# Down projection wholly by seven half-size products, one tile for weight sums, accumulation in DRAM

## The chip, the cores and the metric

One core of one Trainium2 chip runs one launch of the kernel. The metric is device time in microseconds (us).

## The reference

A decoder layer on 512 tokens of width 2048 with an MLP of width 8192, in float32. Cut to what matters:

```python
x = x + jnp.concatenate([attn, ssm], axis=-1) @ w_out[i]
x = x + cross_attention(rms_norm(x, g_cross[i]), rms_norm(mem, g_mem[i]), ...)
hm = rms_norm(x, g_mlp[i])
x = x + jnp.square(jax.nn.relu(hm @ w_up[i])) @ w_down[i]
```

`attn` is a dilated-window attention, `ssm` a chunked state-space scan (SSD); both come out of one input projection of `x`.

## The kernel before, in words

**Arithmetic.** Every float32 operand is split in a high and a low float32r part (ACT copies the high part, DVE subtracts it to get the low one), and a product is three matmuls: high by high, high by low, low by high. For plain products these are lines L212 to L214 (`mm3`), with rows of 512 columns.

**Seven products.** The up projection doesn't multiply 2x2 blocks by eight half-size products but by seven, from sums of the blocks of either operand (Strassen's scheme in Winograd's form). These matmuls have 256 columns (L920 to L922, `up_products`). The operands' sums have to be made and split too: of the weights in `up_forms` (L894 to L911), of the activations in `forms`; the seven results are put together in `combine` (L924), seven DVE operations.

**Stages.** In order of time: input projection, attention and SSD, up to about 690 us; W_out and the cross attention, up to about 1040 us; the up projection, 32 groups `f` of 256 columns, four steps each, a step being the 512 KB of weights that one DMA brings, up to 1666 us; the down projection, up to 2347 us.

**The up projection's step.** SP loads a raw tile `wr` (three buffers, L891). ACT copies three of its four blocks to `wh` (L899), DVE makes four sums of 256 columns (L901 to L904) in `sw`, ACT copies those to `sh` (L905), DVE subtracts: L908 gives `wl` (768 columns), L909 gives `sl` (1024 columns). `wh`, `wl`, `sh`, `sl` have two buffers each. PE then issues 42 matmuls. After four steps ACT copies one of the seven results out of PSUM (L930), DVE combines (L932 to L938), ACT applies relu and square and stores to DRAM.

**The down projection's step.** Its 8192 rows are cut in 8 chunks. Of the 2048 output columns, 0 to 1023 go by seven products (four groups S0 to S3, two steps of 42 matmuls each) and 1024 to 2047 by plain products (two groups P0 and P1 of 512 columns, four steps of 24 matmuls each): 16 steps in a chunk, 128 in all. The list `steps` gives the order. Sums over chunks stay in SBUF: S groups in `accs` by DVE additions (L1128), P groups in `acc`, which starts as the residual from DRAM (`x3d`), by a DVE operation that also scales by the row factor `c2` (L1117). After the last chunk the S groups are combined, transposed on PE (L1158), scaled, added to the residual (L1159) and stored (L1160). A step loads the weights of the step after next (`load_step`), prepares those of the next (`prep_step`), empties the banks of the last (`evac_step`), and multiplies (`mm_step`).

**Memory pools.** `wp` holds the raw, high and low weight tiles of the whole kernel; `bq` holds the 12 scratch tiles (`q`) of attention and SSD and is closed after SSD (`mixer.close()`); `wq`, with the sums of the weights, is opened after that in the place of `bq`. `bp` has the 68 general tiles `b`.

**What sets the order.** A scheduler orders each engine's instructions when the kernel is built; on the chip each engine then runs its own list in that order and waits at the head of it. `weights` has a raised priority (`PRI`).

Of the kernel before, what the change touches and what calls it, by code (L numbers as in the profile page):

```python
# [18 lines left out]
NT = 4  # L19
# [4 lines left out]
DS = 1024  # L24
# [52 lines left out]
def pack_up(w):  # L77


    k, m = w.shape  # L80
    t = w.reshape(k // 512, 2, 2, 128, m // 256, 2, 128).transpose(4, 0, 3, 5, 2, 1, 6)
    return np.ascontiguousarray(np.stack([t[:, :, :, 1, 0], t[:, :, :, 0, 0], t[:, :, :, 0, 1], t[:, :, :, 1, 1]], axis=3))


def pack(inputs):
# [18 lines left out]
        "wds": pack_up(inputs["w_down"][0][:, :DS]),  # L104
        "wdp": pack_rows(inputs["w_down"][0][:, DS:], 512),
# [4 lines left out]
def tile_layer(ctx, tc, vec, x, xT, memT_d, pos, wqk, wv0, wv1, wv2, wzx, wout, wcq, wckv, wco, wup, wds, wdp,  # L110
               out):
# [4 lines left out]
    wp = ctx.enter_context(tc.tile_pool(name="wp", bufs=2))  # L116
# [6 lines left out]
    bq = mixer.enter_context(tc.tile_pool(name="bq", bufs=NBUFQ))  # L123

# [71 lines left out]
    def load(src):  # L196
        a, n = src.shape[1], src.shape[2]
        raw = wp.tile([128, 1024], F32, name="wr", tag="wr", bufs=WR)[:, :a * n]
        nc.sync.dma_start(h3(raw, a), src)
        return raw, a, a * n  # L200

    def weights(src):
        with tc.high_priority(PRI):
            raw, a, n = src if isinstance(src, tuple) else load(src)
            hi = wp.tile([128, 1024], F32R, name="wh", tag="wh", bufs=WH)[:, :n]
            lo = wp.tile([128, 1024], F32R, name="wl", tag="wl", bufs=WH)[:, :n]
# [53 lines left out]
    first = wp.tile([128, 1024], F32, name="wr", tag="wr", bufs=WR)  # L260
# [403 lines left out]
    wq = ctx.enter_context(tc.tile_pool(name="wq", bufs=WQ, reuse_waits="tile"))  # L664
# [7 lines left out]
    x3d = dp.tile([4, 4, 128, 512], F32, name="x3d")  # L672
# [198 lines left out]
    def third_out(n, xr, ps):  # L871
        xs = []
        for t in range(NT):
# [3 lines left out]
            act.dma_start(x3d[t, n], xr[t])  # L877
# [8 lines left out]
    prods = ((0, 0, 0, H0), (1, 1, 0, H1), (2, 6, 1, H0), (3, 3, 1, H1), (4, 4, 2, H0), (5, 5, 2, H1), (6, 2, 3, H0))  # L886
    adr = [dp.tile([128, 512], F32, name=f"a{f}") for f in range(FF // 128)]

    def up_weights(f, q, w=wup):
        raw = wp.tile([128, 1024], F32, name="wr", tag="wr", bufs=WR)  # L890
        nc.sync.dma_start(raw, w[f, q].rearrange("p a b c -> p (a b c)"))  # L891
        return raw

    def up_forms(raw):  # L894
        w21, w11, w12, w22 = (raw[:, 256 * i:256 * i + 256] for i in range(4))
        hi = wp.tile([128, 1024], F32R, name="wh", tag="wh", bufs=WH)
        sw = wq.tile([128, 1024], F32, name="sw", tag="sw")
# [323 lines left out]
```

## Time and profile before

| | before |
|---|---|
| median of 3 runs | 2354.26 us (2353.75 to 2355.12) |
| profiled execution, its own time | 2353.13 us |
| its span, first to last instruction | 2351.1 us |
| PE busy | 2338.1 us, 99% |
| DVE busy | 1686.9 us, 72% |
| ACT busy | 1118.5 us, 48% |
| POOL busy | 13.4 us |
| DMA | 286 MB, 122 GB/s mean |
| mean granted TensorE clock | 1.000 |

PE is the TensorE matmul, PEld its weight load, DVE the VectorE, ACT the ScalarE, POOL the GpSimd, SP the SyncE, which here only issues DMAs. A granted clock of 1.000 is the full 2.4 GHz. Busy shares are means over all stages.

### The profile page before, as it was taken

How to read it: one execution, taken by the hardware profiler on the slowest of the kernel's cores; microseconds unless marked ns; L12 is line 12 of the kernel's file. 1: busy time of each engine (PE TensorE's matmuls, PEld its weight loads, DVE VectorE, ACT ScalarE, POOL GpSimd, SP SyncE). 2: the span in 40 equal slices, each digit the busy share in tenths (PEclk: the TensorE clock that was granted, in tenths of full speed). 3: DMA queues.
4: the chain of work that ended last, by engine and by line, in shares of the span. 5: the costliest groups of instructions: out<-in, count | busy, mean ns of one | idle time of the engine just before them, and what ended most of it. 6: DMA issues, size and time to landing. Idle time of an engine off the chain costs nothing.

```text
span 2351.1 us, 36723 instructions
## 1 busy us (share of the span) xinstructions
PE 2338.1 (99%) x14606; PEld 2077.8 (88%) x14606; DVE 1686.9 (72%) x3100; ACT 1118.5 (48%) x1722; POOL 13.4 (1%) x30
## 2 busy tenths in 40 slices
PE   9999999999999999999999999999999999999999
PEld 8889977777778887789999999999988989889898
DVE  7544276686673346688888888888867887887787
ACT  6334277655452346675444444554543443443332
POOL 0000000000000000000000000000000000000000
PEclk9999999999999999999999999999999999999999
DMA  5222321122224456434443444444543433343344
GB/s 198 90 87 80 99 66 59 54 72 81 74 81 133 160 167 202 135 108 135 133 128 129 132 135 135 131 131 135 187 137 119 140 127 109 132 135 119 117 135 144
DMA packets 98283, 286.22 MB, mean 122 GB/s; under 512 B 11200, under 2 KB 15424, under 8 KB 98112
## 3 DMA queue, kind: packets, MB, share of 16 engines
q1 hardware_dynamic: 82368, 252.42, 33.3%
q10 hardware_dynamic: 13824, 25.17, 2.8%
q0 software_dynamic: 1920, 6.29, 0.9%
q8 instruction: 114, 1.87, 0.3%
q14 instruction: 57, 0.47, 0.1%
HBM read 254.48 MB, written 29.36 MB: 121 GB/s over the span
## 4 chain that ended last, share of the span: by engine, by line
PE 95%; ACT 2%; DVE 2%; issue 1%; DMA 0%; SPq 0%; ACTq 0%; DVEq 0%
PE mm L214 13%; PE mm L212 13%; PE mm L213 13%; PE aux L922 7%; PE mm L922 7%; PE aux L920 7%; PE mm L920 7%; PE aux L921 7%; PE mm L921 7%; PE aux L213 3%; PE aux L214 3%; PE aux L212 3%; PE aux L248 1%; PE aux L523 1%; PE aux L514 1%
## 5 line engine op out<-in xcount | busy, mean ns | idle before, releaser
L208 DVE TENSOR_TENSOR wl<-wr,wh 128x1024 fp32r<-128x1024 f32 (+2 forms) x223 | 264.4, 1186 | 281.7 <-ACT wh L207 280.9
L207 ACT ACTIVATE wh<-wr 128x1024 fp32r<-128x1024 f32 (+2 forms) x223 | 229.3, 1028 | 458.3 <-PE mm L214 250.3
L212 PE MATMUL mm<-wh,b 128*128 128x512 f32 (+2 forms) x1056 | 404.8, 384 | 3.3 <-ACT b L422 1.6
L213 PE MATMUL mm<-wl,b 128*128 128x512 f32 (+2 forms) x1056 | 402.8, 382 | 0.9 <-DVE wl L208 0.7
L214 PE MATMUL mm<-wh,b 128*128 128x512 f32 (+2 forms) x1056 | 402.6, 381 | 0.0
L899 ACT ACTIVATE wh<-wr 128x768 fp32r<-128x768 f32 x192 | 162.5, 846 | 309.4 <-PE mm L921 121.4
L909 DVE TENSOR_TENSOR sl<-sw,sh 128x1024 fp32r<-128x1024 f32 x192 | 234.5, 1221 | 97.1 <-ACT sh L905 96.8
L905 ACT ACTIVATE sh<-sw 128x1024 fp32r<-128x1024 f32 x192 | 203.6, 1061 | 120.3 <-DVE sw L904 37.1
L212 PEld LDWEIGHTS mm<-wh,b 128*128 128x128 f32 x1056 | 198.7, 188 | 42.9 <-ACT b L422 2.0
L213 PEld LDWEIGHTS mm<-wl,b 128*128 128x128 f32 x1056 | 198.8, 188 | 39.8 <-DVE wl L208 2.1
L214 PEld LDWEIGHTS mm<-wh,b 128*128 128x128 f32 x1056 | 198.7, 188 | 38.1 <-issue 0.2
L921 PE MATMUL mm<-b,sh 128*128 128x256 f32 x768 | 217.2, 283 | 0.0
L921 PE MATMUL aux<-b,sh 128*128 128x256 f32 x768 | 217.2, 283 | 0.0
L920 PE MATMUL mm<-b,sh 128*128 128x256 f32 x768 | 217.2, 283 | 0.0
L920 PE MATMUL aux<-b,sh 128*128 128x256 f32 x768 | 217.2, 283 | 0.0
L922 PE MATMUL mm<-b,sl 128*128 128x256 f32 x768 | 216.9, 283 | 0.0
L922 PE MATMUL aux<-b,sl 128*128 128x256 f32 x768 | 216.6, 283 | 0.0
L908 DVE TENSOR_TENSOR wl<-wr,wh 128x768 fp32r<-128x768 f32 x192 | 183.3, 955 | 26.9 <-ACT wh L899 19.8
L922 PE MATMUL aux<-b,wl 128*128 128x256 f32 x576 | 162.1, 282 | 1.2 <-DVE wl L908 1.1
L920 PE MATMUL mm<-b,wh 128*128 128x256 f32 x576 | 162.4, 282 | 0.0
L920 PE MATMUL aux<-b,wh 128*128 128x256 f32 x576 | 162.2, 282 | 0.0
L922 PE MATMUL mm<-b,wl 128*128 128x256 f32 x576 | 162.1, 281 | 0.0
(303 smaller groups left out, 5252.2 us busy)
## 6 DMA issues: line engine op xcount, KB each, us to landing
wr<-in_wup_dram SPq DMA_DIRECT2D x128, 512.0 KB, 3.8
wr<-in_wdp_dram SPq DMA_DIRECT2D x64, 512.0 KB, 3.7
wr<-in_wds_dram SPq DMA_DIRECT2D x64, 512.0 KB, 3.7
wr<-in_wzx_dram SPq DMA_DIRECT2D x48, 512.0 KB, 3.6
wr<-in_wout_dram SPq DMA_DIRECT2D x32, 512.0 KB, 3.8
a<-b ACTq DMA_DIRECT2D x64, 256.0 KB, 4.6
b<-a SPq DMA_DIRECT2D x64, 256.0 KB, 4.4
wr<-in_wqk_dram SPq DMA_DIRECT2D x31, 512.0 KB, 3.6
```

The source lines that it names most:

```text
L207: act.activation(hi, raw, AF.Copy)
L208: dve.tensor_tensor(lo, raw, hi.bitcast(F32), OP.subtract)
L212: pe.matmul(ps, l[0], r[0], start=start, stop=False)
L213: pe.matmul(ps, l[0], r[1], start=False, stop=False)
L214: pe.matmul(ps, l[1], r[0], start=False, stop=stop)
L899: act.activation(hi[:, :768], raw[:, 256:], AF.Copy)
L905: act.activation(shi, sw, AF.Copy)
L908: dve.tensor_tensor(lo[:, :768], raw[:, 256:], hi[:, :768].bitcast(F32), OP.subtract)
L909: dve.tensor_tensor(slo, sw, shi.bitcast(F32), OP.subtract)
L920: pe.matmul(ps[b][:, H], w[0][:, d], xf[0], start=st, stop=False, skip_group_check=True)
L921: pe.matmul(ps[b][:, H], w[0][:, d], xf[1], start=False, stop=False, skip_group_check=True)
L922: pe.matmul(ps[b][:, H], w[1][:, d], xf[0], start=False, stop=sp_, skip_group_check=True)
```

## The change

1. **Down projection.** All eight groups of 256 output columns go by seven products. A chunk has 8 groups of two steps; all 128 steps have 42 matmuls of 256 columns. The plain path is gone. The last two groups of the up projection (f = 30 and 31) are interleaved step by step.
2. **Weights.** `wp` and `wq` give way to one pool `zp`, opened after `mixer.close()`, hence in the memory of `wp` and `bq`: `zr` (three raw tiles of 2048 columns), `zh` and `zl` (two each, 1792 columns). `wp` itself now closes with `mixer`, so that W_out and all later weights use `zr`, `zh`, `zl`. The sums are made in `zr` beside the raw blocks by one add of 512 columns with a broadcast input (L903) and two of 256 (L904, L905). ACT copies 768 (L902) and 1024 columns (L906), and one DVE operation of 1792 columns subtracts all (L907).
3. **Partial sums.** ACT copies the seven results' four banks to SBUF (L1104); GpSimd DMAs add them into `accd` in DRAM (L1106; the first chunk stores, L1108). In the last chunk groups 0 to 5 are read back, combined, transposed (L1143), scaled by ACT (L1144) and added by GpSimd DMAs (L1145) into `out`, where `third_out` has already put the residual; `x3d` is gone. The last two groups (`LATE`) read `accd` early and add on DVE (L1100).
4. **Combination.** `combine` has five DVE operations in place of seven (two of 512 columns with a broadcast input; L928 to L930, L850), and the activations' sums are made by fewer, wider ones.

The core of the diff:

```diff
+    wp = mixer.enter_context(tc.tile_pool(name="wp", bufs=2))
...
     mixer.close()
-    wq = ctx.enter_context(tc.tile_pool(name="wq", bufs=WQ, reuse_waits="tile"))
+    zp = ctx.enter_context(tc.tile_pool(name="zp", bufs=2, reuse_waits="tile"))
+    weight_tile.update(raw=lambda: zp.tile([128, 2048], F32, name="zr", tag="zr", bufs=WR),
+                       hi=lambda: zp.tile([128, 1792], F32R, name="zh", tag="zh", bufs=WH),
+                       lo=lambda: zp.tile([128, 1792], F32R, name="zl", tag="zl", bufs=WH))
...
     def up_forms(raw):
-        act.activation(hi[:, :768], raw[:, 256:], AF.Copy)
-        dve.tensor_tensor(s1, w21, w22, OP.add)
-        dve.tensor_tensor(s2, s1, w11, OP.subtract)
-        dve.tensor_tensor(s3, w11, w21, OP.subtract)
-        dve.tensor_tensor(s4, w12, s2, OP.subtract)
-        act.activation(shi, sw, AF.Copy)
-        dve.tensor_tensor(lo[:, :768], raw[:, 256:], hi[:, :768].bitcast(F32), OP.subtract)
-        dve.tensor_tensor(slo, sw, shi.bitcast(F32), OP.subtract)
+        act.activation(hi[:, 1024:], q(4, 3), AF.Copy)
+        dve.tensor_tensor(h3(q(2, 2), 2), h3(q(4, 2), 2), q(7)[:, None, :].to_broadcast([128, 2, 256]), OP.add)
+        dve.tensor_tensor(q(1), q(2), q(5), OP.add)
+        dve.tensor_tensor(q(0), q(1), q(6), OP.add)
+        act.activation(hi[:, :1024], q(0, 4), AF.Copy)
+        dve.tensor_tensor(lo, q(0, 7), hi.bitcast(F32), OP.subtract)
...
+    def combine(b, copy):
+        dve.tensor_tensor(h3(t1, 2), h3(b[1], 2), p1[:, None, :].to_broadcast([128, 2, 256]), OP.add)
+        dve.tensor_tensor(h3(t2, 2), h3(b[2], 2), t1[:, None, H1].to_broadcast([128, 2, 256]), OP.add)
+        dve.tensor_tensor(t1[:, H1], b[0][:, H1], t2[:, H1], OP.add)
+        stt_(t3[:, H0], t2[:, H0], b[2][:, H1])
+        stt_(t3[:, H1], t2[:, H0], b[3][:, H0])
...
+    steps = [("U", 0, f, q, 4) for q in range(4) for f in (NU - 2, NU - 1)]
+    steps += [("S", c, j, q, FCH // 512) for c in range(NC) for j in range(NJ) for q in range(FCH // 512)]
...
+        elif c == NC - 1 and j >= NJ - LATE:
+            for b, w in enumerate(BW):
+                dve.tensor_tensor(accs[j][b][:, w], ps[b][:, w], accs[j][b][:, w], OP.add)
         else:
+            for b, w in enumerate(BW):
+                o = big()
+                act.activation(o[:, w], ps[b][:, w], AF.Copy)
                 if c:
+                    nc.gpsimd.dma_start(accd[j][b], o[:, w], accum_op=OP.add)
                 else:
+                    nc.gpsimd.dma_start(accd[j][b], o[:, w])
...
+            act.activation(r[:, h], p[:, h], AF.Copy, scale=c2[:, t:t + 1])
+            nc.gpsimd.dma_start(out[t * 128:t * 128 + 128, j * 256:j * 256 + 256], r[:, h], accum_op=OP.add)
```

**Order on PE at the end of SSD.** Before, L640 and L644 (the last block's products) stand among W_out's matmuls (L212 to L214 from `wh`, `wl`):

```order
L640 MATMUL aux<-q 64x128
L212 MATMUL mm<-wh,b 128x512 x3
L213 MATMUL mm<-wl,b 128x512
L214 MATMUL mm<-wh,b 128x512
L213 MATMUL mm<-wl,b 128x512
L640 MATMUL aux<-q 64x128 x3
L644 MATMUL aux<-q 64x128 x2
L640 MATMUL aux<-q 64x128 x2
L644 MATMUL aux<-q 64x128 x2
L640 MATMUL aux<-q 64x128 x2
L644 MATMUL aux<-q 64x128 x2
L214 MATMUL mm<-wh,b 128x512
```

Of the change, the same place:

```order
L608 MATMUL aux<-q,b 128x128 x3
L620 MATMUL aux<-acsT,sel 128x512 x2
L640 MATMUL aux<-q 64x128 x4
L644 MATMUL aux<-q 64x128 x2
L640 MATMUL aux<-q 64x128 x2
L644 MATMUL aux<-q 64x128 x2
L640 MATMUL aux<-q 64x128 x2
L644 MATMUL aux<-q 64x128 x2
L578 MATMUL aux<-b,ones 128x512
L212 MATMUL mm<-zh,b 128x512 x4
L213 MATMUL mm<-zl,b 128x512
L214 MATMUL mm<-zh,b 128x512
```

No matmul of W_out stands ahead of the last SSD product now. The first load of a `zr` tile waits for the last reading of the scratch tiles `q`.

**Order on DVE in the up projection**, of one step f to the next. Before (L901 to L904 sums, L908 and L909 subtractions, L932 to L938 combination; the numbers tell tiles apart):

```order
L932 TENSOR_TENSOR b_12125<-mm_11892,b_12127 128x256
L908 TENSOR_TENSOR wl_12214<-wr_12203,wh_12205 128x768
L933 TENSOR_TENSOR b_12124<-mm_11894,b_12127 128x256
L934 TENSOR_TENSOR b_12124<-mm_11894,b_12124 128x256
L909 TENSOR_TENSOR sl_12215<-sw_12206,sh_12207 128x1024
L935 TENSOR_TENSOR b_12124<-mm_11893,b_12124 128x256
L936 TENSOR_TENSOR b_12126<-mm_11893,b_12124 128x256
L937 TENSOR_TENSOR b_12126<-mm_11893,b_12124 128x256
L938 TENSOR_TENSOR b_12125<-mm_11895,b_12124 128x256
L901 TENSOR_TENSOR sw_12320<-wr_12317 128x256
L903 TENSOR_TENSOR sw_12320<-wr_12317 128x256
L908 TENSOR_TENSOR wl_12271<-wr_12260,wh_12262 128x768
```

Of the change (L903 to L905 sums, L907 the subtraction, L930 and L850 the end of the combination):

```order
L929 TENSOR_TENSOR b_11116<-aux_10905,b_11115 128x512
L907 TENSOR_TENSOR zl_11189<-zr_11186,zh_11188 128x1792
L930 TENSOR_TENSOR b_11115<-aux_10903,b_11116 128x256
L850 SCALAR_TENSOR_TENSOR b_11117<-b_11116,aux_10905 128x256
L850 SCALAR_TENSOR_TENSOR b_11117<-b_11116,aux_10906 128x256
L903 TENSOR_TENSOR zr_11290<-zr_11290 128x512
L904 TENSOR_TENSOR zr_11290<-zr_11290 128x256
L905 TENSOR_TENSOR zr_11290<-zr_11290 128x256
L903 TENSOR_TENSOR zr_11361<-zr_11361 128x512
L904 TENSOR_TENSOR zr_11361<-zr_11361 128x256
L905 TENSOR_TENSOR zr_11361<-zr_11361 128x256
L907 TENSOR_TENSOR zl_11241<-zr_11238,zh_11240 128x1792
```

The tile zr_11361 is the third raw tile after zr_11186, so it has the same buffer, which L907 on zr_11186 (second row) releases. Its sums (L903 to L905) stand ahead of the subtraction that gives zl_11241, the next tile that PE needs. Before, the sums that stand ahead of L908 on wr_12260 are those of the next tile, wr_12317, whose buffer was released a step earlier.

**Order on DVE in the down projection**, of the change, in the first chunk (L187: low parts of activations):

```order
L903 TENSOR_TENSOR zr_19914<-zr_19914 128x512
L187 TENSOR_TENSOR b_19801<-b_19784,b_19800 128x512
L904 TENSOR_TENSOR zr_19914<-zr_19914 128x256
L905 TENSOR_TENSOR zr_19914<-zr_19914 128x256
L903 TENSOR_TENSOR zr_19970<-zr_19970 128x512
L904 TENSOR_TENSOR zr_19970<-zr_19970 128x256
L907 TENSOR_TENSOR zl_19917<-zr_19846,zh_19916 128x1792
L905 TENSOR_TENSOR zr_19970<-zr_19970 128x256
L907 TENSOR_TENSOR zl_19973<-zr_19914,zh_19972 128x1792
```

Again sums of a tile two steps on (zr_19970) stand ahead of the subtraction that gives zl_19917. There are four such places in a chunk of 16 steps.

## Rows read from the trace of the kernel before

**Rows 1.** The page: busy times, and the chain that ended last.
```profile
PE 2338.1 (99%) x14606; PEld 2077.8 (88%) x14606; DVE 1686.9 (72%) x3100; ACT 1118.5 (48%) x1722; POOL 13.4 (1%) x30
...
PE 95%; ACT 2%; DVE 2%; issue 1%; DMA 0%; SPq 0%; ACTq 0%; DVEq 0%
```

**Rows 2.** Timeline of PE, down projection: start, duration (us), engine, line, operation.
```profile
1679.66 0.39 PE L212 MATMUL mm<-wh,b 128*128 128x512 f32 x1
...
1687.79 0.40 PE L214 MATMUL mm<-wh,b 128*128 128x512 f32 x1
1688.03 0.28 PE L920 MATMUL aux<-b,wh 128*128 128x256 f32 x1
...
1689.94 0.28 PE L921 MATMUL aux<-b,sh 128*128 128x256 f32 x1
```

**Rows 3.** Line L930 alone: the copy that follows each up-projection column group.
```profile
L930 ACT ACTIVATE b<-mm x16: 384/384/385, 1044.1 to 1644.1; 128x256 f32<-128x256 f32 x16
```

**Rows 4.** Busy time by window, up projection: PE, PEld, DVE, ACT, POOL, clock, DMA share, GB/s.
```profile
1200.00:1400.00 200.00, 200.00 (x1683) 200.00 (x1682) 166.88 (x311) 99.95 (x131) 0.00 (x0) 1.00 0.41 132
```

**Rows 5.** Lines by form, us 662.8 to 686.1: the last SSD blocks.
```profile
L212 PE MATMUL mm<-wh,b 128*128 128x512 f32 x20 | 8.2, 426 | 0.9 <-ACT wh L207 0.9
L213 PE MATMUL mm<-wl,b 128*128 128x512 f32 x18 | 7.2, 400 | 0.2 <-DVE wl L208 0.2
L214 PE MATMUL mm<-wh,b 128*128 128x512 f32 x17 | 6.8, 400 | 0.0
...
L208 DVE TENSOR_TENSOR wl<-wr,wh 128x1024 fp32r<-128x1024 f32 x4 | 4.9, 1216 | 0.0
```

**Rows 6.** Timeline of us 682 to 696: last SSD product.
```profile
685.68 0.48 PE L644 MATMUL aux<-q 128*64 128x128 f32 x3
```

**Rows 7.** Lines by form, us 1200 to 1600, up projection.
```profile
L909 DVE TENSOR_TENSOR sl<-sw,sh 128x1024 fp32r<-128x1024 f32 x80 | 97.8, 1222 | 52.0 <-ACT sh L905 52.0
...
L905 ACT ACTIVATE sh<-sw 128x1024 fp32r<-128x1024 f32 x80 | 84.9, 1061 | 45.7 <-PE aux L921 18.3 <-PE mm L921 18.1 <-ACT b L944 8.1
L908 DVE TENSOR_TENSOR wl<-wr,wh 128x768 fp32r<-128x768 f32 x80 | 76.6, 957 | 11.8 <-ACT wh L899 7.2
L899 ACT ACTIVATE wh<-wr 128x768 fp32r<-128x768 f32 x81 | 68.6, 847 | 112.7 <-PE mm L921 57.5 <-PE aux L921 55.0
...
L902 DVE TENSOR_TENSOR sw<-sw,wr 128x256 f32<-128x256 f32 x81 | 33.8, 418 | 0.0
```

**Rows 8.** Lines by form, us 620 to 700: an add whose second input is broadcast.
```profile
L602 DVE TENSOR_TENSOR q<-aux,dt 128x512 f32<-128x512 f32 x3 | 2.1, 684 | 2.3 <-PE aux L248 2.3
```

**Rows 9.** Timelines of SP and DVE, us 1788 to 1817; brackets: idle before, releaser.
```profile
1793.69 18.58 SPq L891 DMA_DIRECT2D wr<-in_wds_dram  x4
...
1797.42 0.42 DVE L901 TENSOR_TENSOR sw<-wr 128x256 f32<-128x256 f32 x1 [2.83 <-DMA wr<-in_wds_dram]
```

**Rows 10.** Timeline of ACT and DVE, us 1199 to 1225.
```profile
1204.12 0.38 ACT L930 ACTIVATE b<-mm 128x256 f32<-128x256 f32 x1 [2.22 <-PE mm L922]
...
1209.41 0.41 DVE L901 TENSOR_TENSOR sw<-wr 128x256 f32<-128x256 f32 x1
```

**Rows 11.** DMA issues of the line L891, us 1200 to 1600.
```profile
DMA to landing us min/median/max: 3.3/3.8/6.0
```

**Rows 12.** Lines by form, us 1750 to 2300, down projection.
```profile
L901 DVE TENSOR_TENSOR sw<-wr 128x256 f32<-128x256 f32 x55 | 23.1, 421 | 45.2 <-DMA wr<-in_wds_dram 45.2
```

**Rows 13.** DMA queues, us 1200 to 1600: packets, MB, share of 16 engines.
```profile
q1 hardware_dynamic: 11520, 41.95, 34.1%
q10 hardware_dynamic: 5760, 10.49, 6.8%
```

**Rows 14.** DMA issues by POOL, us 700 to 1200.
```profile
L868 POOL DMA_DIRECT2D b<-x2d x16 | 8.5, 538 | 111.9 <-PE mm L214 70.5 <-PE aux L248 20.5 <-PE mm L834 12.0
```

**Rows 15.** Timeline of us 2326 to 2352: the last DVE operation.
```profile
2347.13 0.75 DVE L1117 SCALAR_TENSOR_TENSOR b<-aux,c,b 128x512 f32<-128x512 f32 x1 [0.65 <-PE aux L214]
```

**Rows 16.** The page, DMA issues: KB each, median us from issue to landing.
```profile
out_dram<-b SPq DMA_DIRECT2D x16, 128.0 KB, 2.0
```

More of the change, by code (lines that the diff above doesn't have):

```diff
@@ L197, in load @@
         a, n = src.shape[1], src.shape[2]
-        raw = wp.tile([128, 1024], F32, name="wr", tag="wr", bufs=WR)[:, :a * n]
+        raw = weight_tile["raw"]()[:, :a * n]
         nc.sync.dma_start(h3(raw, a), src)
@@ L259, in tile_layer @@
     pos_i = cp.tile([128, 4], I32, name="pos_i")
-    first = wp.tile([128, 1024], F32, name="wr", tag="wr", bufs=WR)
+    first = weight_tile["raw"]()
     ahead.append((first, 2, 1024))
@@ L278, in split_h @@
         if i == 0:
-            hi = wp.tile([128, 1024], F32R, name="wh", tag="wh", bufs=WH)
-            lo = wp.tile([128, 1024], F32R, name="wl", tag="wl", bufs=WH)
+            hi = weight_tile["hi"]()
+            lo = weight_tile["lo"]()
             ahead[0] = h3(hi, 2), h3(lo, 2)
@@ L913, in up_bank @@
+        act.activation(hi[:, :1024], q(0, 4), AF.Copy)
+        dve.tensor_tensor(lo, q(0, 7), hi.bitcast(F32), OP.subtract)
+        return [tuple(h3(a[:, 256 * i:256 * i + 256], 2) for a in (hi, lo)) for i in range(7)]
     def up_bank(f):
@@ L1053, in tile_layer @@
     dve.tensor_tensor(c2, c2, v2, OP.mult)
-    LAST = FF // 256 - 1
-    for f in range(1, LAST):
+    NU = FF // 256
+    for f in range(1, NU - 2):
         ps = up_bank(f)
@@ L1063, in tile_layer @@
         up_out(f, ps)
[L1067 to L1075 removed]
+    NC, NP, NJ = FF // FCH, FCH // 256, D // 256
+    steps = [("U", 0, f, q, 4) for q in range(4) for f in (NU - 2, NU - 1)]
+    US = len(steps)
+    steps += [("S", c, j, q, FCH // 512) for c in range(NC) for j in range(NJ) for q in range(FCH // 512)]
+    raws, wts, banks, accs = {}, {}, {}, {}
+    araw, AF_ = {}, {}
+    tags = [0]
+    accd = [[dp.tile([128, 512 if b < 3 else 256], F32, name=f"acc{j}_{b}") for b in range(4)] for j in range(NJ)]
+    BW = [slice(0, 512)] * 3 + [H0]
     def load_step(i):
@@ L1147, in cols_sum @@
     def cols_sum(j):
[L1148 to L1160 removed]
+        o2s[j] = combine(accs.pop(j), False)
@@ L1171, in tile_layer @@
-    for at, fn, j in ((0, cols_sum, 0), (0, cols_sum, 1), (1, cols_sum, 2), (1, cols_out, 0), (2, cols_out, 1),
-                      (2, cols_sum, 3), (3, cols_out, 2), (3, cols_out, 3)):
-        tasks.setdefault(len(steps) - 4 + at, []).append((fn, j))
-    def run_steps(a, b):
-        for i in range(a, b):
-            load_step(i + 2)
-            prep_step(i + 1)
-            for t in tasks.get(i, ()):
-                t[0](*t[1:])
-            evac_step(i - 1)
-            mm_step(i)
+        b = US + per * c
@@ new lines, in tile_layer @@
+        for p, (l, f) in enumerate(((-6, -4), (-5, -3), (-3, -1), (-2, 0)) if c == 0 else ((-15, -14), (-12, -11), (-9, -8), (-6, -5))):
+            task(b + l, a_load, c, p)
+            task(b + f, a_forms, c, p)
+    last = US + per * (NC - 1)
+    for j in range(NJ):
+        end = last + 2 * j + 2
+        if j < NJ - LATE:
+            task(end + 2, acc_load, j)
+            task(end + 3, cols_sum, j)
+            task(end + 4, cols_out, j, 0)
+            task(end + 5, cols_out, j, 1)
+        else:
+            task(end - 2, acc_load, j)
+            task(end + 1, cols_sum, j)
+            task(end + 1, cols_out, j, 0)
+            task(end + 1, cols_out, j, 1)
@@ L1186, in tile_layer @@
     prep_step(0)
-    with tc.manual_schedule():
-        run_steps(0, MAN)
-    run_steps(MAN, len(steps))
-    evac_step(len(steps) - 1)
+    for i in range(len(steps) + 6):
+        load_step(i + 2)
+        prep_step(i + 1)
+        if 0 < i <= len(steps):
+            evac_step(i - 1)
+        for t in tasks.get(i, ()):
+            t[0](*t[1:])
+        if i < len(steps):
+            mm_step(i)
 NBUF = 68
 NBUFQ = 12
-WR, WH, WQ = 3, 2, 2
+WR, WH = 3, 2
 MMB = 4
 WARM = 12
-MAN = 0
+LATE = 2
 PRI = 100
 _ARRAYS = ("vec", "x", "xT", "memT", "pos", "wqk", "wv0", "wv1", "wv2", "wzx", "wout", "wcq", "wckv", "wco",
-           "wup", "wds", "wdp")
+           "wup", "wdn")
 def kernel(**inputs):
```

181 lines of the change are left out of this document (64 added, 117 removed).

## Prediction

> **What bounds the kernel now.** I read the page first, then the windows, the timelines and the lines by form. PE is busy almost without a gap and holds 95% of the chain that ended last [rows 1]. So two things alone can move the time: fewer PE microseconds, or new waits of PE. In the up projection PE has no gap at all, while DVE is busy for 166.88 of 200 us [rows 4]: there is little room on DVE for a wait. The profiled execution took 2353.13 us, 1.1 below the median of 2354.26; the sum below is made against the former. A difference under 0.2%, 4.7 us, I count as no change.
>
> **PE in the down projection: -36.5 us.** 512-column matmuls follow one another at (1687.79 - 1679.66) / 35 = 0.232 us, 256-column ones at (1689.94 - 1688.03) / 16 = 0.119 us [rows 2]. A plain step has 24 of the former, 5.57 us; a seven-product step has 42 of the latter, 5.00 us. The up projection confirms the second: one name's 16 groups stand 600.0 us / 15 = 40.0 us apart, which is two groups of four steps [rows 3]. 64 plain steps become seven-product steps: 64 x 0.57 = 36.5 us saved. Half sizes halve the pitch but for 3%, so the gain is real.
>
> **The end of SSD: +12 us.** Before, 20 + 18 + 17 = 55 matmuls of W_out fill the pauses of the last two SSD blocks, 55 x 0.232 = 12.8 us of work that is done when the last SSD product ends [rows 5, 6]. By the order none of it is there now, because the first `zr` lies in the memory of the scratch tiles and is loaded after their last reading. On the other side four L208, 4.9 us, leave DVE's chain there [rows 5], so that SSD ends about 686.1 - 4.9 = 681.2. A weight load lands 3.8 us after issue [rows 11], the high copy takes 1.06 [rows 7]: W_out's first matmul starts at 686.1, as many matmuls behind as were done there before. I take 12 us, since small stalls that stood in the old overlap (0.9, 0.2) go too. If only the reading of the last scratch tile by DVE, some us earlier, held the load, it would be 10; if SSD were not shortened, 12.8 + 4.9 = 18. While it waits PE is idle for about 5 us. The Trainium skill, "TensorE: Matmul & The Clock Gate" (Part 1), says that an idle TensorE falls to 1.2 GHz and has to be busy before it is given 2.4 again; by that the first matmuls of W_out would follow at twice their pitch and this term would grow by a few us. No row of this trace shows the lower level.
>
> **The up projection: +27 us.** The work of a step changes little: the four sums of 418 ns become one of 512 and two of 256 columns, and two subtractions, 957 + 1222 ns, become one. From 768 to 1024 columns costs 265 ns [rows 7], so 1792 columns take 1222 + 3 x 265 = 2.02 us; a broadcast add of 512 takes 0.68 [rows 8]. What counts is DVE's order: once per f the sums of the tile two steps on stand ahead of the subtraction that PE needs next, and that tile's load waits for the buffer that the subtraction before it frees. I walk it, with the first matmul of that step as zero. ACT: high copy 0.13 to 0.98, result copy (0.38) [rows 10] to 1.26, second high copy to 2.22 [rows 7]. DVE: combination 1.30 to 1.98 and 2.02 to 2.70, then the 1792-column subtraction, 2.62 to 4.65. Only now is the buffer free. From issue to the first sum that uses a load took 1797.42 - 1793.69 = 3.73 us [rows 9]: the sums run from 8.38 to 9.96, and the next subtraction ends at 11.90. PE reaches the next step but one at 10.0 and has 8 products of high parts to do first, 0.95: it wants the low parts at 10.95. So it waits 0.95 us, and 28 values of f repeat the pattern: 27 us. A landing of 3.3 gives 0.55 (15 us), one of 4.4 gives 1.6 (45 us) [rows 11]. Before, the sums ahead of a subtraction were those of the next tile, already loaded: L901 starts there without a wait [rows 10]. The other three steps of an f come out 1 to 2 us early.
>
> **The down projection's order: +30 us.** The same pattern stands four times in a chunk of 16 steps. With a landing of 3.7 each comes out about 0.5 us late: 4 x 8 x 0.5 = 16 us. DVE waits for such loads already before the change, 45.2 us over 55 operations [rows 12], yet with steps that leave it more room. On top come the accumulating DMAs: 0.92 MB in every 10 us, 92 GB/s, which the trace of before doesn't have. Weight loads moved 41.95 MB for 34.1% of the DMA engines in 400 us, stores 10.49 MB for 6.8% [rows 13]. At the two rates 92 GB/s cost 24 to 30%, and double if each byte is moved twice: 48 to 60%, beside the 41% there [rows 4]. Loads that share the engines so often take perhaps 0.4 to 1.0 us longer, and each us is 1 us at 32 places: 13 to 32 us. I take 14, near the lower end, the row of plain transfers: 16 + 14 = 30. The ends: 0 if DVE runs ahead enough, 75 if landings rise by 1.9 us to near the longest of 6.0 [rows 11].
>
> **The tail: +9 us.** Before, the last DVE operation starts at 2347.13 and the span ends 4.0 us after the last matmul [rows 15]. Now follow the last matmul: additions (about 1.7), five dependent operations of `combine` (2 x 0.68 + 3 x 0.42 = 2.6), transposes and scaling (about 1), the eight last GpSimd issues at 8.5 / 16 = 0.53 us [rows 14], 4.2, and a landing, 2.0 for a plain store of that size [rows 16] to 4. In all 12 to 14, so 8 to 10 more; 5 to 14 as ends.
>
> **At nothing.** DVE's additions of partial sums and the residual's loads leave, ACT's copies and POOL's issues come; ACT was idle for half of the up projection [rows 4], and neither ends a wait of PE while the copies find a free `b` tile. If accumulations are late, DVE's activation sums wait for such tiles: that is in the second rival.
>
> **Sum.** -36.5 + 12 + 27 + 30 + 9 = +41.5: 2353.1 + 41.5 = 2394.6, and with the median's 1 us 2395.
>
> **Rivals.**
> (a) *Faster: the sums are not late.* If loads land a little sooner, or DVE has slack that my walk misses, the two order terms are gone: -36.5 + 12 + 9 = -15.5, 2338. It decides at a lateness of about 0.25 us for each of the 28 + 32 places: below that the kernel is faster. For it: each lateness is the small difference of long sums. Against it: the walk uses measured durations, and even a landing of 3.3 leaves 0.55. Chance 0.14, for all ways to a faster kernel.
> (b) *One of the two order terms only*: 2338 + 12 to 27, 2350 to 2365. Chance 0.11, of which 0.05 within 0.2%.
> (c) *DMA becomes the bound in the down projection.* With accumulations that cost twice, 41 + 60% fill the engines; loads land at 6 us, (6.0 - 3.7) x 32 = 74 us late beyond the 16, and late accumulations hold the `b` tiles: 2353 - 36.5 + 12 + 27 + 90 + 9 = 2455. For it: no row shows what an accumulation costs. Against it: the mean share leaves room. The Trainium skill, "Collectives: The Full Stack" (Part 3, the bandwidth ceiling), says that a DMA that adds is slower because it has two sources to read, not because of the add; by that the double share holds and this is the likelier case. No row of this trace shows an accumulation. Chance 0.13.
> (d) *The change doesn't save on PE*: the pitches speak against it; no chance of its own.
> My forecast, 2365 to 2430, has the remaining 0.62.
>
> **Numbers.** The likeliest is 2395. The range 2346 to 2438 leaves out about 0.10 below (most of (a)) and 0.10 above (most of (c)). Faster by over 0.2%: 0.14; within: 0.05; slower: 0.81.
>
> **What would show it.** Down steps of 5.0 us between stalls; a gap of PE of some 5 us near 681 to 686 with no W_out matmul ahead of the last L644; in the up projection groups 21 us apart instead of 20.0, with PE waiting for L907 and DVE's L903 waiting for a DMA; in the down projection landings of 4 to 4.7 us; an end 12 to 14 us behind the last matmul. Groups at 20.0 us would prove my walk wrong; landings of 3.7 with no wait of PE in the down projection would prove the load's price wrong.

## The result and the profile after

The change takes 2490.03 us, median of 4 runs (2481.57 to 2501.33), against 2354.69 for the kernel before (4 runs, 2353.75 to 2356.93): a ratio of 1.0576, 95% interval 1.0528 to 1.0625. It is slower, as forecast, but by 135 us and not by 41, and outside the range (2346 to 2438). The profiled execution, the fastest of the four, took 2481.57 us, span 2479.8; the table below is about it.

Five points of the traces split that span: the ACT copy behind the up projection's first group (L930 before, L926 after), behind its 30th and its 32nd, the last matmul of the down projection, and the end.

| us | before | after | difference | forecast |
|---|---|---|---|---|
| start to first up group | 1044.1 | 1058.7 | +14.6 | +12 |
| 29 further up groups | 580.0 | 610.3 | +30.2 | +27 |
| last two up groups | 42.3 | 48.1 | +5.9 | 0 |
| down projection | 680.7 | 741.0 | +60.3 | -6.5 |
| last matmul to end | 4.0 | 21.7 | +17.7 | +9 |
| span | 2351.1 | 2479.8 | +128.7 | +41.5 |

The page after: busy times, the queues, the chain and the DMA issues (KB each, median us to landing), as [rows 1, 13, 16] show them before.

```profile
PE 2353.8 (95%) x15790; PEld 2153.7 (87%) x15790; DVE 1696.7 (68%) x2640; ACT 1252.8 (51%) x2050; POOL 247.1 (10%) x310
...
q1 hardware_dynamic: 80064, 251.37, 30.5%
q0 software_dynamic: 39936, 67.39, 15.6%
...
PE 56%; DVE 17%; DMA 17%; ACT 5%; issue 4%; POOL 1%; SPq 0%; POOLq 0%; DVEq 0%; ACTq 0%
...
L1106 POOL DMA_DIRECT2D acc<-b x216 | 188.6, 1295 | 422.8 <-ACT b L1104 422.2
...
zr<-in_wup_dram SPq DMA_DIRECT2D x128, 512.0 KB, 3.3
zr<-in_wdn_dram SPq DMA_DIRECT2D x128, 512.0 KB, 5.3
acc<-b POOLq DMA_DIRECT2D x186, 256.0 KB, 6.9
```

PE holds 56% of the chain instead of 95%; DVE and DMA hold 17% each. Weights of the up projection land in 3.3 us, those of the down projection, beside the accumulations (`acc`), in 5.3. An accumulation itself lands after 6.9.

**The end of SSD.** Windows of the change (PE, PEld, DVE, ACT, POOL, granted clock, DMA share, GB/s), then PE's timeline:

```profile
660.00:670.00 10.00, 4.60 (x26) 3.37 (x28) 8.34 (x20) 8.14 (x18) 0.00 (x0) 0.62 0.00 0
...
690.00:695.00 5.00, 5.00 (x17) 3.92 (x17) 4.82 (x8) 1.93 (x4) 0.00 (x0) 0.69 0.55 191
695.00:700.00 5.00, 5.00 (x24) 4.14 (x23) 3.06 (x5) 4.15 (x7) 0.00 (x0) 1.00 0.16 39
```

```profile
657.75 0.39 PE L214 MATMUL mm<-b,wl 128*128 128x512 f32 x1
...
681.65 0.84 PE L644 MATMUL aux<-q 128*64 128x128 f32 x3
...
687.44 2.08 PE L212 MATMUL mm<-zh,b 128*128 128x512 f32 x4 [0.60 <-ACT zh L207]
689.32 0.63 PE L213 MATMUL mm<-zl,b 128*128 128x512 f32 x1
689.74 0.63 PE L214 MATMUL mm<-zh,b 128*128 128x512 f32 x1
...
693.15 0.39 PE L213 MATMUL mm<-zl,b 128*128 128x512 f32 x1
693.38 0.39 PE L214 MATMUL mm<-zh,b 128*128 128x512 f32 x1
```

PE is about half busy, and the granted clock is 0.62 to 0.71 in the stretches between 660 and 695 us, a mean of the levels 1.2 and 2.4 GHz; at the lower one matmuls of 512 columns follow at 0.43 us, after 693.15 at 0.23. W_out begins at 687.44, 1.3 us after the time worked out, but its first 13 matmuls and the last SSD products run at the lower level. So the few us that the Trainium skill ("TensorE: Matmul & The Clock Gate", Part 1) would add for an idle TensorE are there, 13 x (0.43 - 0.23) = 2.6 us by estimate for W_out; but here the clock fell ahead of the gap, while PE was still half busy.

SSD itself did not get shorter. From the last matmul of the input projection (657.75) to the end of the last SSD product (682.49) it takes 24.7 us. Before, it took 23.6 (662.55 to 686.16, the latter in [rows 6]):

```profile
662.55 0.39 PE L214 MATMUL mm<-b,wl 128*128 128x512 f32 x1
```

**The up projection.** DVE's timeline over the place in question (brackets: idle before, releaser), and PE's waits from 1050 to 1660 us (us, times, longest):

```profile
1331.08 2.02 DVE L907 TENSOR_TENSOR zl<-zr,zh 128x1792 fp32r<-128x1792 f32 x1
1333.02 0.42 DVE L930 TENSOR_TENSOR b<-aux,b 128x256 f32<-128x256 f32 x1
...
1336.54 0.69 DVE L903 TENSOR_TENSOR zr<-zr 128x512 f32<-128x512 f32 x1 [0.93 <-DMA zr<-in_wup_dram]
1337.27 0.42 DVE L904 TENSOR_TENSOR zr<-zr 128x256 f32<-128x256 f32 x1
1337.73 0.43 DVE L905 TENSOR_TENSOR zr<-zr 128x256 f32<-128x256 f32 x1
1338.07 2.02 DVE L907 TENSOR_TENSOR zl<-zr,zh 128x1792 fp32r<-128x1792 f32 x1
```

```profile
PE aux L919 <- DVE zl L907: 9.7, 14, 2.0
PE mm L919 <- DVE zl L907: 8.2, 13, 2.4
```

This is the walk as predicted: a subtraction frees the raw tile at 1333.10, the sums that use the next load start at 1336.54, 3.44 us later, and the subtraction that PE wants follows them.

**The down projection.** Windows, then PE's and DVE's waits from 1717 to 2460 us:

```profile
1900.00:2000.00 100.00, 94.21 (x764) 93.20 (x763) 75.05 (x101) 56.37 (x90) 31.45 (x36) 0.98 0.88 203
2000.00:2100.00 100.00, 90.10 (x719) 88.67 (x718) 73.58 (x102) 54.97 (x90) 31.46 (x36) 0.97 0.83 186
```

```profile
PE mm L919 <- DVE zl L907: 26.7, 18, 4.4
PE aux L919 <- DVE zl L907: 26.4, 17, 3.1
```

```profile
DVE zr L903 <- DMA zr<-in_wdn_dram: 119.5, 74, 4.7
```

DMA share is 0.88 and 0.83; in the up projection before it was 0.41 [rows 4]. DVE waits 119.5 us for weights (45.2 before, in the 550 us of [rows 12]) and PE 53.1 us for DVE's subtraction L907, and the granted clock is 0.98 and 0.97 in these windows, 0.96 from 1800 to 2300 us.

### The profile page after: what moved, and what is told of

Read it like the earlier page. It is cut to its first block, busy times and chain, and to the rows that moved or that the text cites. A ratio compares the mean times of both kernels' runs of the same rounds, so it can differ in the third digit from the quotient of the medians.

```text
span 2479.8 us, 39390 instructions
## 1 busy us (share of the span) xinstructions
PE 2353.8 (95%) x15790; PEld 2153.7 (87%) x15790; DVE 1696.7 (68%) x2640; ACT 1252.8 (51%) x2050; POOL 247.1 (10%) x310
## 4 chain that ended last, share of the span: by engine, by line
PE 56%; DVE 17%; DMA 17%; ACT 5%; issue 4%; POOL 1%; SPq 0%; POOLq 0%; DVEq 0%; ACTq 0%
DVE zl L907 10%; PE mm L212 10%; PE mm L214 10%; PE mm L213 10%; DMA zr<-in_wdn_dram 8%; DMA zr<-in_wup_dram 4%; PE aux L919 4%; PE mm L919 3%; PE aux L918 3%; PE aux L917 3%; PE mm L918 3%; PE mm L917 3%; DMA b<-a 2%; DVE zr L903 2%; ACT zh L902 1%
## 5 line engine op out<-in xcount | busy, mean ns | idle before, releaser
L907 DVE TENSOR_TENSOR zl<-zr,zh 128x1792 fp32r<-128x1792 f32 x256 | 516.7, 2020 | 51.4 <-ACT zh L906 50.8
L919 PE MATMUL aux<-b,zl 128*128 128x256 f32 x1792 | 507.1, 289 | 36.4 <-DVE zl L907 36.1
L919 PE MATMUL mm<-b,zl 128*128 128x256 f32 x1792 | 505.7, 287 | 35.1 <-DVE zl L907 34.9
L918 PE MATMUL mm<-b,zh 128*128 128x256 f32 x1792 | 509.2, 286 | 3.4 <-DVE b L187 3.4
L917 PE MATMUL aux<-b,zh 128*128 128x256 f32 x1792 | 511.2, 287 | 0.9 <-ACT zh L902 0.9
L918 PE MATMUL aux<-b,zh 128*128 128x256 f32 x1792 | 510.5, 286 | 0.0
L917 PE MATMUL mm<-b,zh 128*128 128x256 f32 x1792 | 508.4, 286 | 0.2 <-DVE b L930 0.2
L902 ACT ACTIVATE zh<-zr 128x768 fp32r<-128x768 f32 x256 | 215.9, 843 | 571.0 <-PE mm L918 262.2
L919 PEld LDWEIGHTS aux<-b,zl 128*128 128x128 f32 x1792 | 345.6, 195 | 43.7 <-DVE zl L907 43.7
L919 PEld LDWEIGHTS mm<-b,zl 128*128 128x128 f32 x1792 | 344.0, 194 | 42.0 <-DVE zl L907 42.0
L918 PEld LDWEIGHTS mm<-b,zh 128*128 128x128 f32 x1792 | 348.1, 194 | 4.5 <-DVE b L187 4.5
L917 PEld LDWEIGHTS aux<-b,zh 128*128 128x128 f32 x1792 | 350.5, 196 | 1.5 <-ACT zh L902 1.1
L918 PEld LDWEIGHTS aux<-b,zh 128*128 128x128 f32 x1792 | 350.0, 195 | 0.0
L917 PEld LDWEIGHTS mm<-b,zh 128*128 128x128 f32 x1792 | 347.7, 194 | 0.8 <-ACT b L1144 0.4
L903 DVE TENSOR_TENSOR zr<-zr 128x512 f32<-128x512 f32 x256 | 176.5, 689 | 211.3 <-DMA zr<-in_wdn_dram 119.5
L906 ACT ACTIVATE zh<-zr 128x1024 fp32r<-128x1024 f32 x256 | 267.7, 1046 | 5.4 <-DVE zr L905 5.4
L1106 POOL DMA_DIRECT2D acc<-b x216 | 188.6, 1295 | 422.8 <-ACT b L1104 422.2
L208 DVE TENSOR_TENSOR wl<-wr,wh 128x1024 fp32r<-128x1024 f32 (+2 forms) x103 | 117.7, 1143 | 134.0 <-ACT wh L207 133.7
L212 PE MATMUL mm<-wh,b 128*128 128x512 f32 (+2 forms) x448 | 161.7, 362 | 2.8 <-ACT b L422 1.6
L214 PE MATMUL mm<-wh,b 128*128 128x512 f32 (+2 forms) x448 | 161.2, 360 | 0.0
```

Source lines behind the costliest of these rows:

```text
L208: dve.tensor_tensor(lo, raw, hi.bitcast(F32), OP.subtract)
L212: pe.matmul(ps, l[0], r[0], start=start, stop=False)
L214: pe.matmul(ps, l[1], r[0], start=False, stop=stop)
L902: act.activation(hi[:, 1024:], q(4, 3), AF.Copy)
L903: dve.tensor_tensor(h3(q(2, 2), 2), h3(q(4, 2), 2), q(7)[:, None, :].to_broadcast([128, 2, 256]), OP.add)
L906: act.activation(hi[:, :1024], q(0, 4), AF.Copy)
```

## The experiments

Each run but e13 was timed once. The four runs of the change spread over 20 us, so stages of the profiled executions are compared; the down projection, which e3 and e4 leave as it is, took 747.0 and 743.0 us there against 741.0, so 6 us in it are within the spread. e1, e2 and e5 leave the sum over the chunks out.

**e1.** `nc.gpsimd.dma_start(accd[j][b], o[:, w])` for all chunks:

```diff
-                if c:
-                    nc.gpsimd.dma_start(accd[j][b], o[:, w], accum_op=OP.add)
```

> The partial sums of chunks 2 to 8 are stored, not accumulated, so the sum over the chunks is left out; everything else is the change. Theory A (the DMA engines spend about twice the time on an accumulated byte, and weight loads queue behind that): the share of queue q0 in the down projection falls from 50% to 25 to 30%, the median landing of the down projection's weight loads from 5.3 us to 4.3 or less, and the down projection (last up-projection group to last matmul) from 741 us to 675 to 705. Theory B (DVE's order makes it late whatever the landing): it stays above 725 us. Theory C (it is the bytes, not the accumulation): share, landing and time stay within 5% of the change's.

**e2.** The same DMAs only for the first chunk (`if not c:`).

> The DMAs of the partial sums of chunks 2 to 8 are left out (ACT still copies them out of PSUM). Theory A: loads land in 3.3 to 3.6 us as in the up projection, and the down projection takes 643 us of matmuls plus 10 to 30 us of DVE's order: 653 to 673 instead of 741. Theory B (DVE's order): above 720 us.

Measured, with the DMA view from 1800 to 2300 us (queue: packets, MB, share) of the change, of e1 and of e2:

```profile
q0 software_dynamic: 24156, 39.06, 49.7%
q1 hardware_dynamic: 18643, 56.32, 33.8%
...
zr<-in_wdn_dram SPq DMA_DIRECT2D x86, 512.0 KB, 5.4
```

```profile
q1 hardware_dynamic: 20022, 60.42, 37.0%
q0 software_dynamic: 13029, 41.50, 23.0%
...
zr<-in_wdn_dram SPq DMA_DIRECT2D x92, 512.0 KB, 4.1
```

```profile
q1 hardware_dynamic: 20822, 63.33, 38.6%
q0 software_dynamic: 288, 0.92, 0.6%
...
zr<-in_wdn_dram SPq DMA_DIRECT2D x97, 512.0 KB, 3.4
```

The down projection takes 694.4 us in e1 (whole 2436.85) and 665.8 in e2 (2402.58). Theory A holds in both (only e1's share of q0, 23.0%, is below the 25 to 30 expected). Stores cost 28.6 us, adding on top of storing another 46.6, together 75 of the 96 us that the down projection lies above its 128 x 5.04 = 645 us of matmuls. An accumulated MB takes 0.497 x 500 / 39.06 = 6.4 us of the 16 engines, a stored one 0.23 x 500 / 41.5 = 2.8: 2.3 times. "Collectives: The Full Stack" (Part 3, the bandwidth ceiling) of the Trainium skill speaks of two sources to read instead of one; by that an accumulated byte would cost about twice, and these runs show somewhat more.

What the 75 us consist of, by windows over the down projection of the change and of e2, and by PE behind a long wait in the change:

```profile
1717.12:2458.01 740.89, 675.34 (x5365) 665.29 (x5365) 544.41 (x744) 399.31 (x640) 223.09 (x268) 0.97 0.83 199
```

```profile
1713.32:2379.00 665.68, 652.86 (x5365) 646.68 (x5365) 545.71 (x744) 396.81 (x640) 34.19 (x52) 0.99 0.47 147
```

```profile
1861.63 0.58 PE L919 MATMUL aux<-b,zl 128*128 128x256 f32 x1 [3.06 <-DVE zl L907]
1862.01 0.41 PE L917 MATMUL aux<-b,zh 128*128 128x256 f32 x1
1862.22 0.41 PE L918 MATMUL aux<-b,zh 128*128 128x256 f32 x1
```

PE is without work for 65.55 us instead of 12.82, which makes 52.7 of the 75. The other 22.5 are the same 5365 recorded matmuls, which keep PE busy for 675.34 us instead of 652.86, at a mean granted clock of 0.97 instead of 0.99: behind the wait of 3.06 us matmuls of 256 columns follow at 0.21 us instead of 0.12. So a late load costs its wait and, behind a long wait, some time at the lower level too.

**e3.** `mixer.close()`, `zp` and `weight_tile.update(...)` moved to the line ahead of `uw += [up_weights(0, 0), ...`.

> The pool of the new weight tiles is opened just ahead of the up projection, so that W_out and the cross attention use the old weight tiles and nothing waits for the scratch tiles. Theory (the pool's place opens the hole at the end of SSD, and the lower clock behind it): W_out's matmuls stand among the last SSD blocks again, the first up-projection group ends at 1044 to 1046 us as before instead of 1058.7, and the whole gains 12 to 15 us on the change. Rival (the first loads of the new tiles only move the wait to the start of the up projection): the first group still ends after 1053 us.

Measured: whole 2465.3 us; the first group ends at 1037.56, 21.1 us sooner than in the change. The hole cost 19 to 21 us: 1.8 of the 21.1 lie ahead of it, since the last matmul of the input projection starts at 655.93 in e3 and at 657.75 in the change. That is more than was expected, and the first group now ends 6.5 us before that of the kernel before: the new place of the tiles gains time too (e9 to e15).

**e4.** The up projection's loop written with `tc.manual_schedule` on DVE:

```diff
+            if i + 2 < len(uq):
+                up_sums(ur[i + 2])
+            if i + 1 < len(uq):
+                us[i + 1] = up_split(ur[i + 1])
+            if i + 4 < len(uq):
+                ur.append(up_weights(*uq[i + 4]))
+            if done:
+                up_out(*done)
```

> Only in the up projection's groups 1 to 29 DVE's order is written by hand: sums two steps ahead, then the subtraction of the next step, then the combination; tiles and buffers are the change's. Theory (the sums that stand ahead of a subtraction that PE waits for cost about 1 us per group): groups follow at 20.0 to 20.1 us instead of 20.65 to 21.1 and the stage of 29 groups takes 580 to 584 us instead of 610. Rival (three raw buffers or DVE's work itself are too little): still 595 us or more.

Measured: 583.4 us instead of 610.3 for the 29 groups, whole 2458.72. The order was worth 26.9 us. PE's recorded waits for L907 in the change come to 17.9 of these, in 27 places. 27 groups of the change take 20.8 us, 0.7 more than those of e4, and two take 24.3 and 23.9, where PE had waited 2.4 and 2.0 us and the granted clock then was 0.83 over 10 us (1465 to 1475, 1530 to 1540).

**e5 and e6.** The same in the down projection (activation sums in two parts, and nearer to their use, since they share the tiles), together with e3 and e4; e5 without the accumulations.

> Late pool and DVE's order by hand in the up and down projection (activation sums in two parts, closer to their use), and the partial sums' DMAs of chunks 2 to 8 left out. Theory (what is left of the down projection's loss without these DMAs, 665.8 - 643.5 = 22 us, is DVE's order): the down projection takes 643 to 651 us, the whole 2335 to 2350. Rival (it is the amount of DVE's work, which the order can't change): 660 us or more.

> As the run without partial sums, but with the change's accumulating DMAs. Theory (late loads matter only because DVE's order turns each late load into a late subtraction; sums two steps ahead tolerate a landing of about 5.5 us): down projection 655 to 690 us instead of 741, whole 2345 to 2385, median landing still over 5 us. Rival (the DMA engines are full: 0.58 for accumulations at full speed of PE, 0.38 for loads): 710 us or more, DMA share 0.9 or more.

Measured: down projection 667.3 us in e5 (whole 2362.7) and 729.1 in e6 (2424.89, DMA share 0.90, landing 6.0). Both theories fall. Windows of e5, the transition from the up projection and one chunk:

```profile
1674.00:1700.00 26.00, 19.39 (x138) 18.26 (x138) 22.14 (x33) 12.58 (x21) 2.17 (x4) 0.87 0.42 137
...
1834.00:1914.00 80.00, 79.68 (x660) 79.19 (x660) 68.93 (x91) 48.48 (x79) 0.00 (x0) 1.00 0.39 126
```

A chunk keeps PE busy for 79.68 of 80 us, so the order is mended there, and e5's rival (too much work for DVE) isn't seen, though its number is met. A part of the gain is lost again at the transition, where PE is busy for 19.39 of 26 us (the last two up groups take 52.4 us in both runs). The last 91.2 us (2250.0 to 2341.2) hold 719 recorded matmuls, 671 products (a chunk has 672, 80.6 us) and 48 transposes: the end of the down projection costs some 10 us on top of its products. In e2 the order's own loss, PE's waits for L907 in the down projection, is 6.9 + 3.8 = 10.7 us. With nearly full engines the order gained 12 us of the down projection (729.1 instead of 741.0) and left the greater part of the loss: the rival of e6 holds. But in e6 ACT also waits 47.1 us for activations, which are loaded later there; e12 removes that.

**e7.** `SB = (1, 3, 5, 7)`: those groups' partial sums in SBUF, added by DVE.

> As the run with all accumulations and the order by hand, but groups 1, 3, 5 and 7 keep their partial sums in SBUF (DVE adds, 2.15 us each per chunk), so half the accumulated bytes are left. Theory (the accumulated bytes set the loss): share of q0 25 to 29%, landing 4.0 to 4.5 us, down projection 650 to 670 us, whole 2340 to 2365. Rival (DVE's additions take it over the 5 us a step has: 77 of 80 us per chunk): 680 us or more, PE waiting for L923 with DVE busy over 90%.

Measured: 763.6 us (whole 2456.41), though q0's share is 26.5% and the landing 4.5. ACT waits 45.6 us for activations and DVE 42.6 for weights. It was a miss for both: DVE is busy for 85% of the time from 1800 to 2300 us, not for over 90 as the rival has it. The run doesn't tell whether DVE's additions or the late activations cost more.

**e8.** One accumulation of 128 x 1792 per group, `op.tile([128, 1792])`, `accd[j]` of that size.

> As the run with all accumulations and the order by hand, but one accumulating DMA of 128 rows of 1792 columns per group and chunk instead of four of 512 and 256 (the evacuation tile is wider, the pool of general tiles 7 smaller). Theory per byte (an accumulated byte costs a fixed multiple): the time that q0's packets take per MB stays within 10% of the change's (49.7% of 500 us for 39.06 MB, 6.4 us of 16 engines per MB). Theory per packet: it falls by a quarter or more, and so do landing and down projection.

Measured: down projection 715.7 us (whole 2408.28); 47.0% for 41.46 MB, 5.7 us per MB, 11% less than the change's 6.4. That is outside both theories, nearer to the one per byte. In e6, the run that e8 differs from in these rows (and in 7 general tiles less), it was 0.562 x 500 / 40.87 = 6.9: against that it is 18% less, with a landing of 5.2 instead of 6.0 us. So the length of the rows matters too, and the price of an accumulated MB is not the same in every run.

**e12.** As e8, activations loaded 4 to 5 steps earlier, last two groups by DVE and SP.

> All groups by seven products and accumulated in DRAM with one wide DMA each, DVE's order by hand, activations loaded 4 to 5 steps earlier than in the two runs before it, and the last two groups added to the residual by DVE and stored by SP. Theory (in those runs ACT waited for activations that landed after 6 to 7 us, 6 us a chunk; the rest is the load on the DMA engines): chunks of 82 to 85 us instead of 86 to 90, down projection 670 to 695, end 8 to 13 us behind it, whole 2340 to 2375. Rival (the DMA engines are full whatever the order): down projection above 705.

Measured: down projection 721.1 us, whole 2414.2. ACT no longer waits for activations, and still it is no faster: waits of DVE and PE, 1720 to 2440 us:

```profile
DVE zr L911 <- DMA zr<-in_wdn_dram: 84.3, 34, 5.8
```

```profile
PE mm L932 <- DVE zl L920: 21.3, 18, 3.2
PE aux L932 <- DVE zl L920: 9.1, 13, 1.4
```

The rival's number holds, but the engines are not full on the mean (share 0.79 from 1800 to 2300 us). They are for a while: from 1940 to 1945 us the share is 1.00, and DVE waits 5.31 us there for one load. Loads beside accumulations stay late in every order tried. The end behind the last matmul is 16.0 us, 16.6 in e8: the other way out of the last groups gains next to nothing.

**e10.** Parts 2 and 4 of the change with the down projection of before, late pool and order by hand in the up projection.

> The change without its parts 1 and 3: down projection as before (four seven-product groups, two plain ones, partial sums in SBUF, residual apart), but weight tiles and sums of the change, pool opened late, DVE's order by hand in the up projection. Theory (the parts 1 and 3 made the loss, 2 and 4 cost nothing once the hole and the order are mended): first group at 1037 to 1040 us, down projection 672 to 686, end 4 us behind it, whole 2335 to 2352. Rival (the wide tiles hurt the down projection too, by their later release): down projection above 695.

Measured: 2347.13 us, down projection 677.4, end 4.0. As the theory has it, parts 1 and 3 made the loss in the down projection. But that 2 and 4 cost nothing isn't shown: e10's `wp` lies as in e9 and e13 below, and against the 2340.2 to 2343.3 us of that kernel they cost some 4 to 7, most of it up to the first group (1038.4 against 1032.7 in e9).

**e11.** As e10, `("P0", "S0", "S1", "S2", "S3", "S4", "S5")`, `DR = (1, 4)` in DRAM.

> As the run of parts 2 and 4, with six seven-product groups and one plain group of 512 columns; of the six, two (1 and 4) are accumulated in DRAM, four in SBUF. Theory (a quarter of the accumulated bytes leaves the loads on time, and PE's saving of 4 x 8 x 0.5 = 16 us shows): share of q0 13 to 16%, landing under 4 us, down projection 660 to 675, whole 2330 to 2348. Rival (DVE, over 90% of a chunk with its additions): down projection 685 or more, PE waiting for L907's like.

Measured: down projection 722.6 us, whole 2400.64, a miss, although q0's share is 13.9% and the weights land in 3.3 us. ACT waits 34.3 us for activations and DVE 31.1 for their high parts. DVE is busy for 78% (1800 to 2300 us), so the rival's "over 90%" isn't it either. Which of these waits is at the root wasn't followed.

**e9 and e13.** In the kernel before, one line moved:

```diff
-    wp = ctx.enter_context(tc.tile_pool(name="wp", bufs=2))
     dp = ctx.enter_context(tc.tile_pool(name="dp", bufs=1, space=bass.MemoryType.DRAM))
...
     bp = ctx.enter_context(tc.tile_pool(name="bp", bufs=NBUF))
+    wp = ctx.enter_context(tc.tile_pool(name="wp", bufs=2))
     mixer = ExitStack()
```

> The kernel before with one line moved: the pool of the weight tiles is opened after the general tiles, as in the change, so that the tiles lie elsewhere in SBUF; no instruction changes. In the change's trace matmuls of 512 columns follow one another at 0.227 us where before shows 0.232. Theory (where the tiles lie sets that): pitch 0.227 in the input projection and in the plain down steps, whole 10 to 25 us shorter. Rival (something else in the change's run sets it): pitch 0.232, whole within 3 us of before.

> The kernel before with the weight pool opened after the general tiles, timed in five rounds. Theory (the place of the tiles sets the pitch of matmuls, every execution alike): 2339 to 2343 us, 0.45 to 0.65% below before. Rival (that one run was a chance): within 0.2% of before.

Measured: 2340.6 us, and in five rounds 2340.63 (2340.18 to 2343.3) against 2353.86: a ratio of 0.9946, interval 0.9932 to 0.9959. It beats both kernels, by 0.54% the one before. PE, DVE and ACT run the same instructions in the same order in both traces, and in those of e14 and e15. The same stretch of W_out on PE, before and in e13:

```profile
802.25 0.40 PE L214 MATMUL mm<-wh,b 128*128 128x512 f32 x1
802.48 0.40 PE L212 MATMUL mm<-wh,b 128*128 128x512 f32 x1
...
803.88 0.40 PE L212 MATMUL mm<-wh,b 128*128 128x512 f32 x1
```

```profile
802.40 0.39 PE L213 MATMUL mm<-wl,b 128*128 128x512 f32 x1
802.63 0.39 PE L214 MATMUL mm<-wh,b 128*128 128x512 f32 x1
...
803.99 0.39 PE L214 MATMUL mm<-wh,b 128*128 128x512 f32 x1
```

Seven pitches take 1.63 us before (0.233 each) and 1.59 in e13 (0.227).

**e14.** `bp` with `side="right"`. **e15.** `wp` opened ahead of `cp`.

> The kernel before with the pool of general tiles placed from the other end of SBUF; the weight tiles stay where they are, ahead of everything but the constants. No instruction changes. If the place of the weight tiles sets the pitch of the 512-column matmuls: 0.232 us as before, whole 2350 to 2358. If that of the general tiles does: 0.227, whole 2335 to 2346.

> The kernel before with the weight pool opened ahead of the constants, so that the weight tiles lie a few KB lower and the general tiles where they were. If the weight tiles' distance or the general tiles' place sets the pitch: 0.232 us, whole 2350 to 2358. If a few KB are enough (an address within some unit): 0.227 or another pitch, whole off by more than 5 us.

Measured: 2348.58 and 2348.39 us. The pitches near 800 us and in the up projection (about 1300 us):

| | 512 columns | 256 columns | 29 up groups |
|---|---|---|---|
| before | 0.232 | 0.119 | 580.0 us |
| e13 | 0.227 | 0.120 | 584.6 us |
| e14 | 0.233 | 0.118 | 576.2 us |
| e15 | 0.229 | 0.119 | 580.4 us |
| change | 0.227 | 0.120 | 583.4 us (in e4) |

In e14 neither case fits: moving the general tiles leaves the 512-column pitch and changes the 256-column one. In e15 the second case does: a few KB for the weights change the 512-column pitch, and the whole is off by 5.5 us. That the place sets the pitch is shown; by what rule isn't.

## Why the prediction was wrong, point by point

- **PE in the down projection (-36.5):** right. Undisturbed pairs of steps take 10.08 us, so 128 steps take 645 us, 36 less than the 680.7 before.
- **The end of SSD (+12):** the hole is there as forecast, but e3 gives the term 19 to 21 us. SSD was to get 4.9 us shorter without the four L208; it got 1.1 longer (24.7 us against 23.6), and for that case the text itself had 18. TensorE's lower clock, which it named and left out of the sum, adds some 2.6. That W_out's start was forecast to 1.3 us is luck: the input projection ended 4.8 us sooner (657.75 instead of 662.55), by the new place of the tiles, which the prediction didn't consider at all. Up to the first group this place gains 9 to 11 us in e9 and e13, so the stage shows only +14.6. About 5 us more lie between W_out's last matmul and the first group (28.8 us, 28.5 in e3, 23.4 before); no run explains them.
- **The up projection (+27):** the mechanism was right, and the sum too, 26.9 us by e4; but the sum is in part luck. Most groups were late by 0.7 us and not 0.95, and two long waits with the lower clock behind them made up for it. The rest of +30.2 is the pitch of 256 columns, 583.4 against 580.0.
- **The down projection's order (+30):** this is the step that failed. Of it, 16 us were for the order, and e2's waits give about 11. The other 14, "near the lower end, the row of plain transfers", were for the accumulations, and measured 75 (741.0 - 665.8): 52.7 us of longer waits and 22.5 of matmuls at the lower clock, for which the sum had no term. Plain transfers, which the choice went by, cost 28.6 (e1). The upper bound of the engines' share, 48 to 60% with each byte moved twice, was the measured one (49.7%); and 0.4 to 1.0 us longer landings came out as 5.4 - 3.4 = 2.0.
- **Rival (c), 2455:** in kind this is what happened, with 2481.6 in the profiled execution. It had the chance of 0.13 because "the mean share leaves room". At a mean share of 0.84 (1800 to 2300 us) loads were late. Its 90 us for the down projection compare with 96 above the floor; late `b` tiles, which it counted on too, were a small part (9.1 us, below).
- **The tail (+9):** +17.7. POOL is busy for 10.54 us with the last 12 issues (0.88 each); forecast were 8 at 0.53, 4.2 us. From their end at 2472.3 to the end of the span it takes another 7.5 us, where a landing of 2 to 4 was forecast:

```profile
2456.66 0.85 POOL L1145 DMA_DIRECT2D out_dram<-b  x1 [2.24 <-ACT b L1144]
2461.76 10.54 POOL L1145 DMA_DIRECT2D out_dram<-b  x12 [4.25 <-ACT b L1144]
```

- **At nothing:** the transition of the last two up groups cost 5.9 us, and the ACT copies did wait for `b` tiles held by accumulations, 9.1 us in all; that alone is small.

## What to carry to other kernels

Price an accumulating DMA as more than two plain stores in engine time, and add it to the share that the loads beside it already use: DVE waited 67.1 us for weights at a mean share of 0.60 (e1) and 119.5 at 0.84 (1800 to 2300 us), so a mean well below 1 is no proof that loads come on time. A wait of PE can cost more than its length, by the lower clock behind it. A wider in-place tile lives longer, so ask of each wider operation which buffer it now releases late, and what stands in the engine's list between the release and the next use. A pool opened in another pool's place waits for that pool's last reader; opened later, it left no such hole (e3).

## What the runs showed of the hardware that was not expected

Where tiles lie in SBUF changes the pitch of matmuls: 0.227 to 0.233 us for 512 columns and 0.118 to 0.120 for 256, with the same instructions. That was worth 13 us of 2354, as much as the sum's smaller terms (12 and 9). An accumulation with rows of 7 KB took 5.7 us of engine time per MB, with rows of 1 and 2 KB 6.4 (6.9 in e6), and a plain store 2.8.
